# A two-layer decoder trunk on one core: an opening of small ordered transfers, first products in parts, six unread products, and weight casts kept in written order

## The chip, the core and the metric

The kernel runs on one core of a Trainium2 chip. Five engines work side by side, each on its own queue in the order in which its instructions stand: PE multiplies matrices, DVE and ACT work element by element, SP (and here at times ACT) issues transfers, POOL does almost nothing. An instruction waits at the head of its engine's queue until the semaphores that it needs are there, and all behind it wait too. The metric is the device time of one execution in microseconds (us).

## The reference, cut to what matters

256 tokens of width 2048 go through two layers, a pooling mixer and a latent attention, each followed by a gated embedding.

```python
h = x
for i in range(DEPTH):                       # DEPTH = 2
    xn = rms_norm(h, pre_norm[i])
    if i % 2 == 0:
        out = pool_mixer(xn, pool_w_in[j], pool_w_group[j], pool_scale[j], pool_w_out[j])
    else:
        out = mla_mixer(xn, cos, sin, mla_w_in[j], ...)
    h = h + rms_norm(out, post_norm[i])
    gate = jax.nn.sigmoid(rms_norm(h, ple_norm[i]) @ ple_w_gate[i])
    h = h + (p[i] @ ple_w_proj[i]) * gate
```

`pool_mixer` multiplies by `w_in` (2048 x 8192), averages over windows of 2, 4, 8 and 16 tokens, mixes in four groups, gates and multiplies by `w_out`. Everything is float32.

## The kernel before, in words

**Numbers in two parts.** To keep float32 accuracy on a faster multiplication, every operand is split: `hi` is the value rounded to fp32r, `lo` the rest. A product is `hi*x_hi + hi*x_lo` (one instruction of 512 columns, since x_hi and x_lo lie side by side) plus `lo*x_hi` (256 columns).

**Weights.** The 3248 weight tiles of 128 x 128 lie in memory in the order of their use, eight to a chunk, so 406 chunks, called c0 to c405 here. `Weights.load` (L188) brings a chunk into one of four `raw` buffers with one transfer (two for c0 and c1). `cut` rounds it on ACT into the upper half of one of eight `hl` buffers; `finish` subtracts on DVE for the lower half. When `take` reaches a new chunk, it emits further loads and casts; a cast is written up to six chunks ahead of use, and `W.rate` says how many are written at each new chunk. A load waits until the subtraction of four chunks earlier has freed its buffer.

**Order.** A list scheduler lays down the instructions of each engine. PE's products always keep their written order. ACT and DVE keep it only where `in_order(True)` is in force: in the opening and around the changes of stage. Elsewhere the scheduler may bring a cast forward, past evacuations that are written earlier.

**Opening.** The input x lies transposed in 16 tiles x0 to x15 of 128 x 256. The first stage takes 16 steps k, each with four output columns m: `split` makes x_k's hi (ACT) and lo (DVE) with the gain column from `vs`, and eight products follow. So one chunk serves two steps. The transfers of x0, `vs`, c0, x1, x2 and x3, c1 and so on are issued by SP, those of x8 to x15 by ACT between its other work.

**After it.** Columns m = 4, 5 and 6 of the same stage follow as whole rows of 32 products each (two chunks). Between them the sum of squares becomes `rstd` (two transposes on PE, copied by ACT). Until `rstd` is there, seven columns wait in the eight PSUM buffers. Then `pooled` (L381) takes each: an ACT copy, and on DVE an add, a product with rstd into `u`, the window sums `win`, an edge product, the mean `tmp`, and the split (ACT cast, DVE subtraction). The gate stage of each layer (at the end of `mixer_end`) has the same form: eight columns wait for its rstd, and each then takes an add, two products and an add on DVE and a sigmoid on ACT, in layer 0 also a split for the next layer.

**End.** The last column m = 15 of the last gate needs c404 and c405; `linear_short` takes three products of 256 columns for each of 16 tiles.

Of the kernel before, what the change touches and what calls it, by code (L numbers as in the profile page):

```python
# [9 lines left out]
F32 = mybir.dt.float32  # L10
F32R = mybir.dt.float32r
I32 = mybir.dt.int32
AF = mybir.ActivationFunctionType
ALU = mybir.AluOpType
AX = mybir.AxisListType

P = 128
D = 2048
T = 256
KD = D // P  # L20
# [16 lines left out]
CH = 8  # L37
SLOTS = 52
N_TILES = 3248
KO_POOL = 4  # L40
RUN = 16
KO_GATE = 5
N_FREE = 2
KO_LAT = 5
# [71 lines left out]


@with_exitstack
def tile_trunk(ctx: ExitStack, tc: tile.TileContext, ws, xp, pp, pos, vec, cst, outT):
    nc = tc.nc  # L120
    n_chunks = ws.shape[0]

# [1 line left out]
    wp = ctx.enter_context(tc.tile_pool(name="wp", bufs=1))  # L124
# [5 lines left out]
    def nm(s):  # L130
        uid[0] += 1
        return f"{s}_{uid[0]}"
# [13 lines left out]
            return emit  # L146

    pe, act, dve = InOrder(nc.tensor, True), InOrder(nc.scalar, False), InOrder(nc.vector, False)

    def in_order(on):  # L150
        act.on = dve.on = on

    def act_tile(dt=F32R):
        return ap.tile([P, 2 * T], dt, tag="act", name=nm("act"), bufs=SLOTS)
# [14 lines left out]
    def tmp_tile():  # L169
        return own_tile("tmp", 6)  # L170

    def ps_tile():
        return psp.tile([P, 2 * T], F32, tag="ps", name=nm("ps"))

    class Weights:
# [10 lines left out]
            self.rate = 2  # L186

        def load(self):  # L188
            c = self.loaded
            self.loaded += 1  # L190
            t = self.raw[c] = wp.tile([P, CH * P], F32, tag="raw", name=nm("raw"), bufs=4)
            for r in self.pieces(c):
                nc.sync.dma_start(t[:, r], ws[c][:, r])  # L193

        def cut(self):

            c = self.cut_to
            self.cut_to += 1
            hl = self.hl[c] = wp.tile([P, 2, CH * P], F32R, tag="hl", name=nm("hl"), bufs=8)
            for r in self.pieces(c):  # L200
                act.copy(hl[:, 0, r], self.raw[c][:, r])
            self.finish(c - 1)

        def finish(self, c):
            t = self.raw.pop(c, None)
            if t is not None:
                hl = self.hl[c]
                for r in self.pieces(c):
                    dve.tensor_tensor(hl[:, 1, r], t[:, r], hl[:, 0, r].bitcast(F32), ALU.subtract)

        def pieces(self, c):
            n = 2 if c < 2 else 1
            s = CH * P // n
            return [slice(i * s, (i + 1) * s) for i in range(n)]

# [6 lines left out]
        def take(self, *tiles):  # L222
            c, j = divmod(len(self.order), CH)
            n = len(tiles)
            assert j + n <= CH
            if j == 0:
                self.hl.pop(c - 1, None)
                while self.loaded < min(n_chunks, c + self.AHEAD_LOAD + 1):
                    self.load()
                while self.cut_to <= c:  # L230
                    self.cut()
                self.finish(c)
                self.run_ahead(self.rate)
            self.order += tiles
            r = slice(j * P, (j + n) * P)
            return self.hl[c][:, 0, r], self.hl[c][:, 1, r]

    W = Weights()

    vs = one.tile([P, NV], F32, name="vs")  # L240
    cs = one.tile([P, NK], F32, name="cs")
    ident = cs[:, K_ID : K_ID + P]
    ones = one.tile([P, P], F32, name="ones")
# [6 lines left out]
    def col(i):  # L250
        return vs[:, i : i + 1]

    def split(src, gain=None):
        t = act_tile()
        if gain is None:
            act.copy(t[:, :T], src)
            dve.tensor_tensor(t[:, T:], src, t[:, :T].bitcast(F32), ALU.subtract)
        else:
            act.activation(t[:, :T], src, AF.Copy, scale=gain)
            dve.scalar_tensor_tensor(  # L260
                t[:, T:], src, gain, t[:, :T].bitcast(F32), ALU.mult, ALU.subtract
            )
# [12 lines left out]
    def linear(xs, name, m, between=None):  # L275

        ps = ps_tile()
        n = len(xs)
        for a in range(0, n, RUN):
            burst(  # L280
                [(ps, xs[k], (name, k, m), k == 0, k == n - 1) for k in range(a, min(n, a + RUN))],
                between if a + RUN >= n else None,
            )
        return ps
# [16 lines left out]
    def outer_step(pss, x, name, k, n):  # L301
        burst([(ps, x, (name, k, m), k == 0, k == n - 1) for m, ps in enumerate(pss)])

    def whole(ps, out):
        t = tmp_tile()
        act.copy(t, ps[:, T:])
        dve.tensor_tensor(out, ps[:, :T], t, ALU.add)
        return out
# [46 lines left out]

    in_order(True)
    W.rate = 0
    early = one.tile([P, 1], F32, name="early")
    act.activation(early, mean_d, AF.Copy, scale=mean_r)
    x_t = []  # L360

    def load_x(queue, j):
        t = act_tile(F32)
        x_t.extend([t[:, :T], t[:, T:]])
        queue.dma_start(t, xp[:, 2 * j : 2 * j + 2, :])  # L365

    t = act_tile(F32)
    x_t += [t[:, :T], t[:, T:]]
    nc.sync.dma_start(t[:, :T], xp[:, 0, :])  # L369
    nc.sync.dma_start(vs, vec)  # L370
    W.load()
    nc.sync.dma_start(t[:, T:], xp[:, 1, :])  # L372
    for j in range(1, 4):
        load_x(nc.sync, j)
        W.load()

    u_buf = [one.tile([P, PAD + T], F32, name=f"u{i}") for i in range(2)]
    for t in u_buf:
# [30 lines left out]
        return s  # L409

    xs, pss = [], [ps_tile() for _ in range(KO_POOL)]
    for k in range(KD):
        xs.append(split(x_t[k], col(V_PRE[0] + k)))
        outer_step(pss, xs[k], "pool_in", k, KD)
        if len(x_t) < D // P:
            load_x(act, len(x_t) // 2)
        if k == KD // 2:
            nc.sync.dma_start(cs, cst)
        if k == 12:
            W.rate = 1  # L420
    acc = [own_tile("acc", 4) for _ in range(2)]
# [8 lines left out]
    for g in range(4):  # L430
# [18 lines left out]
        for i in range(8):  # L449
            ps = linear(pl, f"mix{g}", i)  # L450
            t = whole(ps, tmp_tile())
# [41 lines left out]
    def mixer_end(layer, src, h, pss):  # L493
# [43 lines left out]
        for i in range(KD + 2):  # L537
# [11 lines left out]
            if i >= 2:  # L549
                k = i - 2  # L550
                if k == 0:
                    pss = [ps_tile() for _ in range(KO_GATE)]
                dve.scalar_tensor_tensor(
# [50 lines left out]
    h, xs = mixer_end(0, gated, None, [])  # L604
# [12 lines left out]
    pss = [ps_tile() for _ in range(KO_LAT)]  # L617
# [37 lines left out]
    t = whole(linear(xs, "kpe", 0), tmp_tile())  # L655
# [131 lines left out]
    pss = None  # L787
# [9 lines left out]
    for i in range(H + 4):  # L797
# [5 lines left out]
        else:  # L803
            if i == H:
                pss = [ps_tile() for _ in range(KO_OUT)]
# [47 lines left out]
```

## Time and profile before

| what | us |
|---|---|
| median of 3 runs (1186.89 to 1188.99) | 1187.14 |
| the profiled execution's own time | 1186.3 |
| its span, first to last instruction | 1184.5 |
| PE busy | 1173.6 |
| PE's first product starts at | 5.86 |
| PE's last products end at | 1179.85 |

A row of a timeline gives the start, the time, the engine, the line, the operation, out<-in with the names of the program, the shapes, how many instructions are merged, and in brackets the idle time before it and what ended that. A row of a table of stretches gives from:to, the length, then busy us and (x) the instructions of PE, PEld, DVE, ACT and POOL, then the granted clock of PE (1.00 is the upper of its two levels), the DMA engines' busy share and GB/s. A row of the waits gives who waits, for whom, the total, how often, and the longest. Nearly all work stands at L142, the helper that records each operation, so rows are told apart by their tiles: `hl<-raw` is the work on weights, `act<-act,vs` a split with a gain, `ps` a PSUM buffer.

### The profile page before, as it was taken

Reading aid. Unit: us, or ns where it says so; the run is one execution under the profiler, and the core shown is the slowest. Engines: PE = TensorE matmul, PEld = TensorE weight load, DVE = VectorE, ACT = ScalarE, POOL = GpSimd, SP = SyncE. Lnnn points to the kernel's source line nnn. Section 1 sums busy time; section 2 is a strip of 40 time slices with the busy share of each in tenths; the row PEclk is TensorE's granted clock in tenths of the full one; section 3 lists DMA queues with packets and bytes.
Section 4 is the critical chain, followed back from the end, with each engine's and each line's share of the span. In section 5 each row is a group of like instructions: output and inputs, shape, how many; then the busy total and the mean of one; then the engine's idle time right before and its main releaser. Section 6 shows DMA issues by size and latency. Waiting matters only on the chain.

```text
span 1184.5 us, 18609 instructions
## 1 busy us (share of the span) xinstructions
PE 1173.6 (99%) x6928; PEld 1042.1 (88%) x6928; DVE 882.5 (75%) x1651; ACT 691.7 (58%) x1240; POOL 1.2 (0%) x10
## 2 busy tenths in 40 slices
PE   7999999999999999999999999999999999999998
PEld 6888888888888888888889889888888889889887
DVE  6888885788588866447446999678788897656995
ACT  7657454554554455445444776557787775655762
POOL 0000000000000000000000000000000000000000
PEclk9999999999999999999999999999999999999999
DMA  8766655655665665675662676655555443562681
GB/s 297 250 210 196 185 189 182 198 189 180 195 192 181 193 198 182 200 268 181 190 196 95 196 252 198 190 178 170 193 188 179 141 124 127 183 193 97 196 275 45
DMA packets 64363, 221.30 MB, mean 187 GB/s; under 512 B 7153, under 2 KB 9841, under 8 KB 64273
## 3 DMA queue, kind: packets, MB, share of 16 engines
q1 hardware_dynamic: 63648, 218.94, 58.4%
q8 instruction: 54, 0.88, 0.3%
q10 hardware_dynamic: 576, 1.05, 0.2%
q14 instruction: 37, 0.29, 0.1%
q0 software_dynamic: 48, 0.13, 0.0%
HBM read 217.99 MB, written 2.10 MB: 186 GB/s over the span
## 4 chain that ended last, share of the span: by engine, by line
PE 97%; DVE 1%; DMA 1%; ACT 0%; SPq 0%; issue 0%; ACTq 0%; DVEq 0%
PE ps L142 97%; DMA raw<-ws 1%; DVE act L142 1%; DVE hl L142 0%; ACT hl L142 0%; SPq L193 0%; SPq L365 0%; DVE tmp L142 0%; ACT tmp L142 0%; ACT act L142 0%; DVE mx L142 0%; SPq L372 0%; SPq L370 0%; SPq L369 0%; ACTq L142 0%
## 5 line engine op out<-in xcount | busy, mean ns | idle before, releaser
L142 PE MATMUL ps<-act,hl 128*128 128x256 f32 (+1 forms) x6512 | 1120.5, 334 | 6.0 <-ACT hl L142 5.9
L142 PEld LDWEIGHTS ps<-act,hl 128*128 128x128 f32 x6512 | 989.0, 190 | 131.7 <-ACT hl L142 6.2
L142 DVE TENSOR_TENSOR hl<-raw,hl 128x1024 fp32r<-128x1024 f32 (+1 forms) x408 | 493.6, 1217 | 223.8 <-ACT hl L142 222.2
L142 ACT CAST hl<-raw 128x1024 fp32r<-128x1024 f32 (+1 forms) x408 | 421.9, 1045 | 282.2 <-PE ps L142 252.7
L142 ACT COPY tmp<-ps 128x256 f32<-128x256 f32 x221 | 80.4, 368 | 61.6 <-PE ps L142 61.4
L142 DVE TENSOR_TENSOR tmp<-ps,tmp 128x256 f32<-128x256 f32 x155 | 64.7, 420 | 16.0 <-ACT tmp L142 15.4
L142 ACT ACTIVATE act<-act,vs 128x256 fp32r<-128x256 f32 (+1 forms) x102 | 50.8, 507 | 27.9 <-DVE act L142 23.3
L142 ACT CAST act<-tmp 128x256 fp32r<-128x256 f32 (+1 forms) x96 | 39.1, 407 | 25.0 <-DVE tmp L142 23.0
L142 DVE TENSOR_TENSOR acc<-acc,tmp 128x256 f32<-128x256 f32 x92 | 35.9, 421 | 14.1 <-ACT tmp L142 13.9
L142 ACT ACTIVATE tmp<-act 128x256 f32<-128x256 f32 x90 | 34.5, 414 | 14.1 <-DVE act L142 14.0
L142 ACT ACTIVATE act<-tmp 128x256 f32<-128x256 f32 x48 | 19.8, 416 | 36.7 <-DVE tmp L142 36.5
L142 DVE TENSOR_TENSOR act<-tmp,act 128x256 fp32r<-128x256 f32 (+1 forms) x96 | 40.2, 419 | 0.9
L142 DVE SCALAR_TENSOR_TENSOR act<-act,vs,act 128x256 fp32r<-128x256 f32 x72 | 33.8, 481 | 6.2 <-ACT act L142 6.2
L142 DVE TENSOR_TENSOR tmp<-tmp,rstd 128x256 f32<-128x256 f32 x74 | 30.9, 420 | 0.3
L142 PE MATMUL ps<-act,act 128*128 128x256 f32 (+1 forms) x224 | 30.6, 291 | 0.0
L142 DVE TENSOR_TENSOR act<-ps,tmp 128x256 f32<-128x256 f32 x66 | 27.3, 419 | 3.4 <-ACT tmp L142 3.1
L142 PEld LDWEIGHTS ps<-act,act 128*128 128x128 f32 x224 | 27.3, 190 | 0.3 <-DVE act L142 0.2
L142 DVE TENSOR_TENSOR act<-act,tmp 128x256 f32<-128x256 f32 (+1 forms) x65 | 26.7, 416 | 0.1
L142 PE MATMUL ps<-hl,act 128*128 128x512 f32 x96 | 22.5, 390 | 0.0
L142 DVE TENSOR_TENSOR win<-win 128x269 f32<-128x269 f32 (+2 forms) x48 | 20.9, 435 | 1.3
L142 PEld LDWEIGHTS ps<-hl,act 128*128 128x128 f32 x96 | 17.8, 188 | 3.5
L142 ACT COPY act<-ps 128x256 f32<-128x256 f32 (+2 forms) x52 | 17.9, 357 | 3.8 <-PE ps L142 3.5
(64 smaller groups left out, 300.3 us busy)
## 6 DMA issues: line engine op xcount, KB each, us to landing
raw<-ws SPq DMA_DIRECT2D x404, 512.0 KB, 4.0
act<-xp SPq DMA_DIRECT2D x11, 256.0 KB, 6.1
outT<-act SPq DMA_DIRECT2D x15, 128.0 KB, 1.7
raw<-ws SPq DMA_DIRECT2D x4, 256.0 KB, 4.2
act<-xp ACTq DMA_DIRECT2D x4, 256.0 KB, 7.2
act<-pp SPq DMA_DIRECT2D x2, 256.0 KB, 4.7
act<-xp SPq DMA_DIRECT2D x2, 128.0 KB, 3.3
cs<-cst SPq DMA_DIRECT2D x1, 206.0 KB, 7.6
```

Source lines behind the costliest of these rows:

```text
L142: i = getattr(self.engine, op)(*a, **k)
```

## The change

The casts and subtractions of weights go through two recorders of their own (`w_act`, `w_dve`) that are always in written order. SP's opening transfers are in written order too. x0 and all gains come in one array `first`, issued by ACT: first x0 with its gain column, then all columns into `vs`. All of x now goes by SP, between the chunks. c0 comes in four pieces, c1 to c5 in two each, and c0 to c5 land in twelve tiles of the pool of activations, so that the four `raw` buffers start with c6. For c0 and c1 the casts and subtractions are written where their products need them, c0's first two casts on DVE. Step 0 is written in parts: hi with x_hi, hi with x_lo, then lo. Ahead of it six products of a tile of ones go to a PSUM buffer that is not read.

```diff
+N_BORROW = 6
+N_HALVED = 2
+N_WARM = 6
...
+    sp = InOrder(nc.sync, True)
+    w_act, w_dve = InOrder(nc.scalar, True), InOrder(nc.vector, True)
...
         def load(self):
             c = self.loaded
             self.loaded += 1
-            t = self.raw[c] = wp.tile([P, CH * P], F32, tag="raw", name=nm("raw"), bufs=4)
-            for r in self.pieces(c):
-                nc.sync.dma_start(t[:, r], ws[c][:, r])
+            if c < N_BORROW:
+                slots = [act_tile(F32) for _ in range(2)]
+                parts = [slots[r.start // (4 * P)][:, r.start % (4 * P) :][:, : r.stop - r.start] for r in self.pieces(c)]
+            else:
+                t = wp.tile([P, CH * P], F32, tag="raw", name=nm("raw"), bufs=4)
+                parts = [t[:, r] for r in self.pieces(c)]
+            self.raw[c] = parts
+            for r, t in zip(self.pieces(c), parts):
+                sp.dma_start(t, ws[c][:, r])
...
-            for r in self.pieces(c):
-                act.copy(hl[:, 0, r], self.raw[c][:, r])
+            if c < N_HALVED:
+                return
+            for r, t in zip(self.pieces(c), self.raw[c]):
+                w_act.copy(hl[:, 0, r], t)
             self.finish(c - 1)
 
         def finish(self, c):
...
+            for r, t in zip(self.pieces(c), self.raw.pop(c, ())):
+                w_dve.tensor_tensor(self.hl[c][:, 1, r], t, self.hl[c][:, 0, r].bitcast(F32), ALU.subtract)
...
         def pieces(self, c):
-            n = 2 if c < 2 else 1
+            n = 4 if c == 0 else 2 if c < N_BORROW else 1
...
+    act.dma_start(x0[:, : T + 1], first[:, : T + 1])
+    act.dma_start(vs, first[:, T:])
...
+    for j in range(1, KD // 2):
+        load_x(j)
         W.load()
+    sp.dma_start(cs, cst)
+    sp.on = False
+    warm = ps_tile()
+    for _ in range(N_WARM):
+        pe.matmul(warm[:, :P], ones, ones, start=True, stop=True)
...
+        for i in range(2):
+            W.first_part(0, i, dve.tensor_copy)
+        gain = x0[:, T : T + 1]
+        act.activation(x[:, :T], x_t[0], AF.Copy, scale=gain)
+        dve.scalar_tensor_tensor(x[:, T:], x_t[0], gain, x[:, :T].bitcast(F32), ALU.mult, ALU.subtract)
+        for i in range(2):
+            W.second_part(0, i)
+        for h in range(2):
+            for ps, (hi, _) in zip(pss, steps):
+                pe.matmul(ps[:, h * T : h * T + T], hi, x[:, h * T : h * T + T], start=h == 0, stop=False)
+        for ps, (_, lo) in zip(pss, steps):
+            pe.matmul(ps[:, :T], lo, x[:, :T], start=False, stop=False)
```

PE's order is the same from step 1 to the end. ACT's and DVE's is not, in the whole program. Three places follow.

The first is ACT behind the first `rstd`, before the change. `CAST hl` rows are chunks: hl_522 is c18, hl_656 is c19, hl_659 c20; `COPY tmp` and `CAST act` belong to `pooled`.

```order
L142 CAST hl_522<-raw_447 128x1024
L142 CAST hl_656<-raw_452 128x1024
L142 COPY rstd_544<-ps_541 128x256
L142 CAST hl_659<-raw_515 128x1024
L142 CAST hl_664<-raw_520 128x1024
L142 COPY tmp_576<-ps_102 128x256
L142 CAST act_572<-tmp_570 128x256
L142 CAST hl_715<-raw_654 128x1024
```

The same place after the change, where hl_558 is c18 and hl_692 is c19; the four pairs of `COPY tmp` and `CAST act` that are left out are of the columns between.

```order
L145 CAST hl_558<-raw_483 128x1024
L145 COPY rstd_580<-ps_577 128x256
L145 COPY tmp_612<-ps_139 128x256
L145 CAST act_608<-tmp_606 128x256
...
L145 COPY tmp_677<-ps_550 128x256
L145 CAST act_673<-tmp_671 128x256
L145 COPY tmp_736<-ps_689 128x256
L145 CAST act_686<-tmp_684 128x256
L145 CAST hl_692<-raw_488 128x1024
L145 CAST hl_695<-raw_551 128x1024
```

The cast of c19 stood ahead of rstd's copy; now it stands behind the split of all seven columns that waited for rstd. DVE there goes from one column to the next without a subtraction of weights in between: its last `TENSOR_TENSOR hl` before the seven is c17's.

The second is ACT in layer 0's gate, behind the copy of its second rstd: before the change, where hl_7048 is c249.

```order
L142 CAST hl_6922<-raw_6847 128x1024
L142 COPY rstd_6944<-ps_6941 128x256
L142 CAST hl_7048<-raw_6852 128x1024
L142 COPY tmp_6979<-ps_6404 128x256
L142 COPY tmp_6990<-ps_6405 128x256
L142 CAST hl_7051<-raw_6915 128x1024
L142 ACT_TABLE_LOAD
```

And after it, where hl_7084 is c249; the 24 rows left out are copies, sigmoids, splits and squares of eight columns.

```order
L145 CAST hl_6958<-raw_6883 128x1024
L145 COPY rstd_6980<-ps_6977 128x256
L145 COPY tmp_7015<-ps_6440 128x256
L145 COPY tmp_7026<-ps_6441 128x256
L145 ACT_TABLE_LOAD
...
L145 ACTIVATE act_7077<-act_5304,vs 128x256
L145 CAST hl_7084<-raw_6888 128x1024
```

c249's cast went from the place right behind rstd to the place behind the split of the eighth column. On DVE 39 instructions of these columns (33 of them TENSOR_TENSOR, 6 SCALAR_TENSOR_TENSOR) stand from rstd to the sum that this split reads.

The third is DVE at the end. Before the change the subtraction of the last chunk c405 (hl_12313) stands among the work of columns 9 to 12.

```order
L142 TENSOR_TENSOR tmp_12097<-act_11438,tmp_12097 128x256
L142 TENSOR_TENSOR tmp_12204<-tmp_12204,rstd_12013 128x256
L142 TENSOR_TENSOR hl_12313<-raw_12263,hl_12313 128x1024
L142 TENSOR_TENSOR tmp_12256<-ps_12257,tmp_12300 128x256
L142 TENSOR_TENSOR tmp_12152<-act_11438,tmp_12152 128x256
```

After the change c405 is hl_12349.

```order
L145 TENSOR_TENSOR tmp_12434<-ps_12435,tmp_12468 128x256
L145 TENSOR_TENSOR tmp_12434<-tmp_12434,rstd_12049 128x256
L145 TENSOR_TENSOR tmp_12434<-act_11878,tmp_12434 128x256
L145 TENSOR_TENSOR act_5312<-act_5312,tmp_12434 128x256
L145 TENSOR_TENSOR hl_12349<-raw_12299,hl_12349 128x1024
L145 TENSOR_TENSOR tmp_12476<-ps_12477,rstd_12049 128x128 x2
```

It moved behind the four instructions of column 14, the last but one, which wait for that column's products.

## Rows read from the trace of the kernel before

**Rows 1.** The page, busy time of each engine, share of the span, instructions.

```profile
PE 1173.6 (99%) x6928; PEld 1042.1 (88%) x6928; DVE 882.5 (75%) x1651; ACT 691.7 (58%) x1240; POOL 1.2 (0%) x10
```

**Rows 2.** Waits of PE's weight loads: who, for whom, total, times, longest.

```profile
PEld ps L142 <- ACT hl L142: 6.2, 2, 5.9
PEld ps L142 <- DVE act L142: 1.0, 4, 0.3
```

**Rows 3.** Timeline of the opening, all engines.

```profile
3.23 0.51 ACT L142 ACTIVATE act<-act,vs 128x256 fp32r<-128x256 f32 x1 [0.90 <-DMA vs<-vec]
...
5.19 1.32 ACT L142 CAST hl<-raw 128x512 fp32r<-128x512 f32 x2 [1.46 <-DMA raw<-ws]
...
5.86 34.16 PE L142 MATMUL ps<-act,hl 128*128 128x512 f32 x176 [5.86 <-ACT hl L142]
...
6.94 0.51 ACT L142 ACTIVATE act<-act,vs 128x256 fp32r<-128x256 f32 x1 [0.43 <-DMA act<-xp]
```

**Rows 4.** Two stretches of 3.4 us: busy time and instructions of each engine, clock, DMA.

```profile
5.86:9.26 3.40, 3.40 (x10) 2.92 (x11) 2.58 (x5) 2.43 (x5) 0.00 (x0) 1.00 0.86 270
9.26:12.66 3.40, 3.40 (x20) 2.92 (x20) 1.70 (x4) 1.47 (x4) 0.00 (x0) 1.00 1.03 402
```

**Rows 5.** ACT's timeline at the first rstd.

```profile
45.78 1.05 ACT L142 CAST hl<-raw 128x1024 fp32r<-128x1024 f32 x1 [0.24 <-DMA raw<-ws]
47.05 1.05 ACT L142 CAST hl<-raw 128x1024 fp32r<-128x1024 f32 x1 [0.21 <-DMA raw<-ws]
48.00 0.36 ACT L142 COPY rstd<-ps 128x256 f32<-128x256 f32 x1
```

**Rows 6.** PE's timeline: the transposes of the first rstd.

```profile
45.88 0.38 PE L142 MATMUL ps<-cs,small 128*128 128x128 f32 x2
```

**Rows 7.** Two stretches from a rstd on, columns as in rows 4.

```profile
46.00:60.98 14.98, 14.98 (x91) 13.35 (x90) 13.56 (x24) 9.03 (x14) 0.00 (x0) 1.00 0.77 258
688.92:703.89 14.97, 14.97 (x91) 13.35 (x90) 14.42 (x26) 13.26 (x24) 0.00 (x0) 1.00 0.78 265
```

**Rows 8.** Timeline of pooled columns, ACT and DVE.

```profile
54.02 0.42 DVE L142 TENSOR_TENSOR tmp<-ps,tmp 128x256 f32<-128x256 f32 x1
54.14 0.41 ACT L142 CAST act<-tmp 128x256 fp32r<-128x256 f32 x1 [1.36 <-DVE tmp L142]
54.45 1.04 ACT L142 CAST hl<-raw 128x1024 fp32r<-128x1024 f32 x1
...
55.81 0.43 DVE L142 SCALAR_TENSOR_TENSOR tmp<-win,u 128x256 f32<-128x256 f32 x1
56.16 1.22 DVE L142 TENSOR_TENSOR hl<-raw,hl 128x1024 fp32r<-128x1024 f32 x1
...
59.09 0.42 DVE L142 TENSOR_TENSOR u<-tmp,rstd 128x256 f32<-128x256 f32 x1
...
60.56 1.22 DVE L142 TENSOR_TENSOR hl<-raw,hl 128x1024 fp32r<-128x1024 f32 x1
```

**Rows 9.** ACT's timeline behind layer 0's second rstd.

```profile
689.20 0.37 ACT L142 COPY rstd<-ps 128x256 f32<-128x256 f32 x1 [0.42 <-PE ps L142]
...
692.55 1.28 ACT L142 ACT_TABLE_LOAD   x1
693.85 0.73 ACT L142 ACTIVATE tmp<-tmp 128x256 f32<-128x256 f32 x2
```

**Rows 10.** DVE's timeline a few us later.

```profile
701.06 0.42 DVE L142 TENSOR_TENSOR tmp<-ps,tmp 128x256 f32<-128x256 f32 x1
701.39 0.88 DVE L142 SCALAR_TENSOR_TENSOR act<-act,vs,act 128x256 fp32r<-128x256 f32 x2
```

**Rows 11.** Timeline of the end, ACT and DVE.

```profile
1174.17 0.37 ACT L142 COPY tmp<-ps 128x256 f32<-128x256 f32 x1 [3.88 <-PE ps L142]
...
1176.41 0.43 DVE L142 TENSOR_TENSOR act<-act,tmp 128x256 f32<-128x256 f32 x1
1179.88 0.49 DVE L142 TENSOR_TENSOR tmp<-ps,rstd 128x128 f32<-128x128 f32 x2 [3.04 <-PE ps L142]
```

More of the change, by code (lines that the diff above doesn't have):

```diff
@@ L118, in tile_trunk @@
 @with_exitstack
-def tile_trunk(ctx: ExitStack, tc: tile.TileContext, ws, xp, pp, pos, vec, cst, outT):
+def tile_trunk(ctx: ExitStack, tc: tile.TileContext, ws, xp, first, pp, pos, cst, outT):
     nc = tc.nc
@@ L199, in cut, with first_part, second_part @@
             hl = self.hl[c] = wp.tile([P, 2, CH * P], F32R, tag="hl", name=nm("hl"), bufs=8)
-            for r in self.pieces(c):
-                act.copy(hl[:, 0, r], self.raw[c][:, r])
+            if c < N_HALVED:
+                return
+            for r, t in zip(self.pieces(c), self.raw[c]):
+                w_act.copy(hl[:, 0, r], t)
             self.finish(c - 1)
         def finish(self, c):
[L205 to L209, printed above, removed]
+            if c < N_HALVED:
+                return
+            for r, t in zip(self.pieces(c), self.raw.pop(c, ())):
+                w_dve.tensor_tensor(self.hl[c][:, 1, r], t, self.hl[c][:, 0, r].bitcast(F32), ALU.subtract)
+        def first_part(self, c, i, copy):
+            copy(self.hl[c][:, 0, self.pieces(c)[i]], self.raw[c][i])
+        def second_part(self, c, i):
+            r = self.pieces(c)[i]
+            dve.tensor_tensor(self.hl[c][:, 1, r], self.raw[c][i], self.hl[c][:, 0, r].bitcast(F32), ALU.subtract)
         def pieces(self, c):
-            n = 2 if c < 2 else 1
+            n = 4 if c == 0 else 2 if c < N_BORROW else 1
             s = CH * P // n
@@ L233, in take @@
                 self.run_ahead(self.rate)
+            if 0 < c < N_HALVED and j % (CH // 2) == 0:
+                self.first_part(c, j // (CH // 2), act.copy)
+                self.second_part(c, j // (CH // 2))
             self.order += tiles
@@ L357, in tile_trunk, with load_x @@
     W.rate = 0
+    x0, t = act_tile(F32), act_tile(F32)
+    act.dma_start(x0[:, : T + 1], first[:, : T + 1])
+    act.dma_start(vs, first[:, T:])
     early = one.tile([P, 1], F32, name="early")
     act.activation(early, mean_d, AF.Copy, scale=mean_r)
-    x_t = []
-    def load_x(queue, j):
+    x_t = [x0[:, :T], t[:, T:]]
+    def load_x(j):
         t = act_tile(F32)
         x_t.extend([t[:, :T], t[:, T:]])
[L365 to L370, printed above, removed]
+        sp.dma_start(t, xp[:, 2 * j : 2 * j + 2, :])
     W.load()
-    nc.sync.dma_start(t[:, T:], xp[:, 1, :])
-    for j in range(1, 4):
-        load_x(nc.sync, j)
+    sp.dma_start(t[:, T:], xp[:, 1, :])
+    for j in range(1, KD // 2):
+        load_x(j)
         W.load()
+    sp.dma_start(cs, cst)
[3 more added lines that the diff above has]
+        pe.matmul(warm[:, :P], ones, ones, start=True, stop=True)
     u_buf = [one.tile([P, PAD + T], F32, name=f"u{i}") for i in range(2)]
@@ L411, in tile_trunk, with first_step @@
     xs, pss = [], [ps_tile() for _ in range(KO_POOL)]
+    def first_step():
+        x = act_tile()
+        steps = [W.take(("pool_in", 0, m)) for m in range(KO_POOL)]
+        for i in range(2):
[10 more added lines that the diff above has]
+            pe.matmul(ps[:, :T], lo, x[:, :T], start=False, stop=False)
+        return x
     for k in range(KD):
+        if k == 0:
+            xs.append(first_step())
+            continue
         xs.append(split(x_t[k], col(V_PRE[0] + k)))
+        if k == 1:
+            for i in range(2, 4):
+                W.first_part(0, i, act.copy)
+                W.second_part(0, i)
         outer_step(pss, xs[k], "pool_in", k, KD)
[L415 to L418, printed above, removed]
         if k == 12:
@@ L834 @@
         "xp": np.ascontiguousarray(a["x"][0].T.reshape(KD, P, T).transpose(1, 0, 2)),
+        "first": np.ascontiguousarray(np.concatenate([a["x"][0].T[:P]] + [vec(x) for x in vecs], 1)),
         "pp": np.ascontiguousarray(a["p"][:, 0].transpose(0, 2, 1).reshape(2, 2, P, T).transpose(0, 2, 1, 3)),
         "pos": np.ascontiguousarray(a["positions"].reshape(T)),
-        "vec": np.ascontiguousarray(np.concatenate([vec(x) for x in vecs], 1)),
         "cst": _consts(),
```

## The prediction

> **What bounds the kernel now.** I read the page first: PE is busy 1173.6 of a span of 1184.5 us [rows 1]. The reader should see that all other time is to be found in about 11 us, so I looked for each idle stretch of PE. The table of waits shows two of its weight loads waiting for a cast of weights, together 6.2, the longest 5.9; that is the start of the program, with 0.3 a little later. Four waits for DVE's `act`, 1.0 in all, stand in the attention [rows 2]. The timeline of the opening shows why PE starts at 5.86: x0's split could go only at 3.23, behind `vs`, and c0's first cast at 5.19, behind its transfer [rows 3]. The stretches behind it show a second loss: PE is busy throughout both, yet does 10 products in the first 3.40 us and 20 in the next. [...] Last comes the tail: PE's last products end just before 1179.88, and DVE and ACT finish up to 1184.5 [rows 1, 11]. So there is little to win, and anything that makes PE wait for ACT or DVE costs its full length.
>
> **The opening.** New are a transfer of x0 with its gain column, a first quarter of c0, and hi/lo products apart. Today data that were issued first were there by 3.23 [rows 3]; a split takes 0.51 [rows 3], so PE's first product can stand at about 3.7, against 5.86: 2.2 earlier. With the wait of 0.3 behind it [rows 2], which the quarters should end, G = 2.4. The lower end is 1.0: the first stretch moved only 270 GB/s against 402 in the next [rows 4], and the bytes ahead of x1, whose split ran at 6.94 on arrival [rows 3], are as many as before, so a start at 3.7 may buy waits at steps 1 and 2. [...]
>
> **Place 1, the cast of c19.** The rows of the order show it moved behind the splits of all seven columns that waited for rstd. PE's order is unchanged, and c19's first product stood at 60.98: 91 products lie from 46.00 to it, the first three of them already begun [rows 7]. When can it stand now? I count from DVE's first `u` behind rstd. The rest of the first column takes 60.56 - 59.09 = 1.47, a whole column 56.16 - 54.02 = 2.14, and six follow. The last column's split needs its STT, which starts 0.35 before the column's end and takes 0.43; ACT's split passes to the next cast after 0.31, and a cast takes 1.05 [rows 5, 8]. A hand-over between engines I estimate at 0.04, twice. 1.47 + 12.84 - 0.35 + 0.43 + 0.31 + 1.05 + 0.08 = 15.8.
>
> The clock of that sum starts at rstd's copy, which has to wait for two things. One is the transposes: 45.88 + 0.38 = 46.26 today [rows 6], minus G after the change. With 0.04 + 0.36 + 0.04, u stands at 46.70 - G and the product at 62.5 - G: a loss of 1.5 - G against 60.98. The other is c18's cast, which stands ahead of the copy on ACT. Today it began at 45.78 after waiting for its transfer, and its successors follow 0.95 later (47.05 to 48.00) [rows 5]. If it begins D earlier, the copy starts at 46.73 - D, u at 47.13 - D and the product at 62.95 - D: a loss of 2.0 - D. The larger of the two holds. So the opening's gain is kept only if c18's transfer moves with it. That transfer waits for a buffer that c14's subtraction frees, and so back by fours to c6, which starts free now. Each link still has a transfer, a cast and a subtraction that the change does not shorten. D lies between -0.7 (c14's cast now queues behind a copy of 0.36 and a split of 0.31 [rows 5, 8]) and 2.4 (it moves with PE). I choose 0.7, nearer to the end at which the transfer sets the pace, since that is what the row of 45.78 names. Net: 2.0 - 0.7 = **+1.3**, from -0.9 (1.5 - 2.4) to +2.7. It is the position of PE after both opening and wait; the wait itself would be G + 1.3 = 3.7 long.
>
> **Place 2, the cast of c249.** The copy of rstd ran at 689.20 for 0.37, so DVE begins at 689.61 [rows 9]. The 39 instructions ahead of the split: 33 at 0.33 (701.06 to 701.39), and 6 at 0.40 (two in 0.88, less 0.09 of overlap) [rows 10], 10.9 + 2.4 = 13.3. After four of them, at 690.9, DVE needs the first sigmoid: on ACT two copies (0.3 each, between a copy's 0.37 and a split's 0.31), the table load of 1.28 and a sigmoid of 0.42 (0.73 for two [rows 9]) follow the rstd copy, to 691.9. That is 1.0 of waiting. 689.61 + 13.3 + 1.0 = 703.9; then the split 0.51 [rows 3], the cast 1.05 [rows 5] and hand-overs 0.08, 705.5. Needed is 703.89 [rows 7]. PE waits **1.6**, counted from the same rstd, so that nothing earlier or later in the program changes it. Bounds: 0.6 if the sigmoid is not waited for, 2.2 if DVE waits half a table load, 0.6, once more among ACT's other 24 instructions.
>
> **Attention.** Some weight subtractions now stand behind the scalings of the softmax, so `act` for PE may come earlier or weights later. What waits there today is 1.0 [rows 2]. I take 0, bounds -1.0 and +1.0 (the same wait, changed to weights).
>
> **Place 3, the end.** The subtraction of c405 stands behind column 14's last add, 1176.41, which passes on after 0.33 [rows 10, 11]; with 1.22 of its own [rows 8] it ends at 1177.97 and PE can go on at 1178.0. The 48 products of column 15 took from the copy of column 14 (1174.17) to DVE's first read (1179.88), 0.119 each [rows 11]. The first product began about 0.2 before that copy; 24 for c404 and two of hi later c405's lower half is needed at 1173.97 + 26 x 0.119 = 1177.1. PE waits **0.9** (0.7 to 1.0), with nothing behind it to hide that.
>
> Everywhere else the casts are written up to six chunks ahead of PE, so that a few places' shift on ACT (58% busy) or DVE (75%) [rows 1] lies behind PE's products: 0.
>
> **Sum.** 1.3 + 1.6 + 0 + 0.9 = +3.8. The profiled execution took 1186.3, so 1190.1; the median, 1187.14, lies 0.84 above that execution, and I keep that: **1190.9**. A measurement of this kernel can tell about 0.2%, 2.4 us, from no change.
>
> **The rivals.**
>
> *The early start survives place 1* (not slower). If the borrowed tiles let c6 to c18 come as much earlier as PE does, D is over 2.05, rstd's copy goes with the transposes, and place 1 gives 1.5 - 2.4 = -0.9. Then -0.9 + 1.6 + 0.9 = +1.6: 1188.7, within 0.2%. For it: the cast of c18 waited only for a transfer [rows 5], and the DMA engines were 0.77 busy there [rows 7]. Against it: three buffers' rounds lie between.
>
> *The columns are quicker than rows 8 say* (faster). Then neither place 1 nor 2 waits and G stays: -2.4 - 1.0 (attention) + 0.9 = -2.5, 1184.6. It needs 3.7 us less in seven columns, 0.5 of 2.14 each; the six DVE instructions of a column fill 2.0 at 0.33 each [rows 10], which speaks strongly against.
>
> *The clock falls back.* The first products ran at half pace after PE had idled for 5.86 [rows 3, 4]. Were a wait of 3.7 at place 1 enough for that, 1.7 comes on top: 1192.6. The waits of up to 0.3 that the trace has elsewhere [rows 2] don't decide it. [...]
>
> *The opening doesn't deliver.* If waits at steps 1 and 2 eat the start, G is about 0 and the transposes would give place 1 +1.5, but D is then near 0, so place 1 gives 2.0 and the sum is 2.0 + 1.6 + 0.9 = +4.5: 1191.6. For it: the low DMA rate of the first stretch [rows 4]. Against it: x1's transfer has no more bytes ahead than today.
>
> **How the numbers follow.** Forecast 0.50 (its own range 1189.3 to 1192.5, of it 0.05 within 0.2%); early start survives 0.24; clock falls back 0.10; opening doesn't deliver 0.09; quicker columns 0.07. Faster: 0.07. Within 0.2%: 0.24 + 0.05 = 0.29. Slower: 0.45 + 0.10 + 0.09 = 0.64. For the range, the bounds that can come together: low, the early start with 1.6 less for the attention and place 2 together, 1187.1; high, the clock case with 1.2 more at the places, 1193.8. I write 1187.0 to 1193.8; the quick columns and the tails left out hold under 2 in 10.
>
> **What would show it.** Right: a first product at about 3.7; one wait of PE for a cast near 58 to 62 of some 3.7 us, whose chunk's cast on ACT stands right behind a split; one near 705 of 1.6; one for DVE's `hl` of 0.9 just before the last products. If the copy of rstd runs well before 46, the early start survives. Ten instead of twenty products in the 3.4 us behind the wait show the clock. The forecast is wrong if ACT's casts there wait for nothing, if the wait at place 1 is missing, or if the opening starts later than 4.6.

## The result and the profile after

The changed kernel took 1194.46 us (median, 1193.44 to 1197.6) against 1187.09 of the kernel before: ratio 1.0066, 95% interval 1.0055 to 1.0078, so 7.4 us slower. The prediction was 1190.9 in a range of 1187.0 to 1193.8: the right direction, half of the size, and outside the range. Its first profiled execution took 1197.6, the longest of the four; a second profiled execution of the same code, told among the experiments, took 1193.6. I read both, since they differ in what matters.

The waits of PE's weight loads in the changed kernel, to be set against [rows 2]:

```profile
PEld ps L145 <- ACT hl L145: 10.0, 4, 4.9
PEld ps L145 <- DVE act L145: 1.3, 5, 0.6
PEld ps L145 <- DVE hl L145: 1.0, 1, 1.0
```

The 5.9 of the start is gone, yet casts cost more than before: two long waits in the middle of the program. The wait for a lower half (`DVE hl`) is the one at the end. The kernel before had one such wait too, in a row that [rows 2] leave out; it lay in the opening, at 14.62:

```profile
PEld ps L142 <- DVE hl L142: 0.5, 1, 0.5
```

The opening in the timeline, against [rows 3]:

```profile
3.56 0.51 ACT L145 ACTIVATE act<-act 128x256 fp32r<-128x256 f32 x1 [0.31 <-DMA act<-first]
...
4.12 2.64 PE L145 MATMUL ps<-act,hl 128*128 128x256 f32 x12 [0.20 <-ACT act L145]
...
5.91 0.51 ACT L145 ACTIVATE act<-act,vs 128x256 fp32r<-128x256 f32 x1 [1.84 <-DMA act<-xp]
...
7.08 3.22 PE L145 MATMUL ps<-act,hl 128*128 128x512 f32 x16 [0.31 <-ACT hl L145]
...
10.45 0.62 ACT L145 CAST hl<-act 128x512 fp32r<-128x512 f32 x1 [1.46 <-DMA act<-ws]
...
11.12 2.14 PE L145 MATMUL ps<-act,hl 128*128 128x512 f32 x10 [0.82 <-ACT hl L145]
```

PE starts at 4.12 instead of 5.86, but then waits for casts ahead of 7.08 and 11.12; the cast at 10.45 had itself waited for the second half of c1, where the kernel before had cast all of c1 by 9.52:

```profile
8.38 1.14 ACT L142 CAST hl<-raw 128x512 fp32r<-128x512 f32 x2
```

The transposes of the first rstd tell what is left. They stood at 45.88 [rows 6] and now start at 45.39, so 0.5 us of the gain remains:

```profile
45.39 0.40 PE L145 MATMUL ps<-cs,small 128*128 128x128 f32 x2 [0.22 <-issue]
```

ACT around the first rstd, against [rows 5] (the left-out rows are the columns' copies and splits):

```profile
45.50 1.05 ACT L145 CAST hl<-raw 128x1024 fp32r<-128x1024 f32 x1 [3.50 <-DMA raw<-ws]
46.73 1.05 ACT L145 CAST hl<-raw 128x1024 fp32r<-128x1024 f32 x1 [0.19 <-DMA raw<-ws]
47.94 1.06 ACT L145 CAST hl<-raw 128x1024 fp32r<-128x1024 f32 x1 [0.15 <-DMA raw<-ws]
48.90 0.36 ACT L145 COPY rstd<-ps 128x256 f32<-128x256 f32 x1
...
63.76 0.41 ACT L145 CAST act<-tmp 128x256 fp32r<-128x256 f32 x1 [1.46 <-DVE tmp L145]
64.07 2.94 ACT L145 CAST hl<-raw 128x1024 fp32r<-128x1024 f32 x3
```

The three casts at the top are c16, c17 and c18, each on the arrival of its transfer. c18 began at 47.94, 2.16 later than before the change; rstd's copy stands right behind it, and c19's cast (64.07) behind the seventh split.

Two more rows tell where a part of this delay comes from: the cast of c8, and the issue of c18's load by SP. First the changed kernel, then the kernel before, where c8 is the second of the two casts and starts at 23.77.

```profile
25.53 1.05 ACT L145 CAST hl<-raw 128x1024 fp32r<-128x1024 f32 x1 [1.97 <-DMA raw<-ws]
...
41.18 0.33 SPq L145 DMA_DIRECT2D raw<-ws  x1
```

```profile
22.84 1.99 ACT L142 CAST hl<-raw 128x1024 fp32r<-128x1024 f32 x2
...
40.54 0.33 SPq L193 DMA_DIRECT2D raw<-ws  x1
```

c18's load went out 0.64 later than before, and 6.76 passed from its issue to the cast instead of 5.24.

PE behind c19's cast, and stretches of 3.4 us behind it, against [rows 7]:

```profile
65.17 1.22 PE L145 MATMUL ps<-act,hl 128*128 128x512 f32 x2 [4.48 <-ACT hl L145]
```

```profile
65.17:68.57 3.40, 3.40 (x8) 2.72 (x9) 3.40 (x5) 2.11 (x3) 0.00 (x0) 0.50 0.40 93
68.57:71.97 3.40, 3.40 (x19) 3.26 (x19) 3.33 (x8) 1.45 (x2) 0.00 (x0) 0.62 0.90 322
```

c19's first product stood at 60.98 and now stands at 65.17: +4.19. Behind the wait of 4.48 the granted clock is 0.50, the lower of the two values that it takes in this trace: it reads 1.00 from 60 to 64.0, 0.50 from 64.5 to 70.67, and 1.00 again from 71.17. In the first 3.4 us PE is busy all the time and does 8 products.

ACT at layer 0's gate, against [rows 9]:

```profile
696.92 1.05 ACT L145 CAST hl<-raw 128x1024 fp32r<-128x1024 f32 x1 [0.66 <-DMA raw<-ws]
697.87 0.36 ACT L145 COPY rstd<-ps 128x256 f32<-128x256 f32 x1
...
712.75 0.51 ACT L145 ACTIVATE act<-act,vs 128x256 fp32r<-128x256 f32 x1 [0.56 <-DVE act L145]
713.17 2.93 ACT L145 CAST hl<-raw 128x1024 fp32r<-128x1024 f32 x3
```

PE's row there:

```profile
714.25 0.96 PE L145 MATMUL ps<-act,hl 128*128 128x512 f32 x3 [3.18 <-ACT hl L145]
```

Before the change this copy waited for PE ([rows 9], "0.42 <-PE ps"). Now it comes directly behind a cast (c248) that waited for its transfer.

The end, against [rows 11], DVE and then PE:

```profile
1186.55 0.42 DVE L145 TENSOR_TENSOR act<-act,tmp 128x256 f32<-128x256 f32 x1
1186.90 1.22 DVE L145 TENSOR_TENSOR hl<-raw,hl 128x1024 fp32r<-128x1024 f32 x1
1191.10 0.49 DVE L145 TENSOR_TENSOR tmp<-ps,rstd 128x128 f32<-128x128 f32 x2 [2.98 <-PE ps L145]
```

```profile
1188.17 2.89 PE L145 MATMUL ps<-act,hl 128*128 128x256 f32 x22 [0.82 <-DVE hl L145]
```

The subtraction of c405 follows column 14's add after 0.35, and PE waits 0.82 for it.

### The profile page after: what moved, and what is told of

Its sections match the earlier page's. It is cut to its first block, busy times and chain, and to the rows that moved or that the text cites. A ratio compares the mean times of both kernels' runs of the same rounds, so it can differ in the third digit from the quotient of the medians.

```text
span 1195.7 us, 18457 instructions
## 1 busy us (share of the span) xinstructions
PE 1179.6 (99%) x6944; PEld 1046.9 (88%) x6944; DVE 887.9 (74%) x1659; ACT 693.1 (58%) x1244; POOL 1.2 (0%) x10
## 4 chain that ended last, share of the span: by engine, by line
PE 88%; DVE 5%; DMA 3%; ACT 2%; issue 1%; SPq 0%; DVEq 0%; ACTq 0%
PE ps L145 88%; DMA raw<-ws 2%; DVE act L145 2%; DVE tmp L145 2%; DVE hl L145 1%; ACT hl L145 1%; ACT tmp L145 1%; DMA act<-ws 1%; DMA act<-xp 0%; DVE win L145 0%; ACT act L145 0%; DVE acc L145 0%; DVE u L145 0%; DMA act<-first 0%; ACT L145 0%
## 5 line engine op out<-in xcount | busy, mean ns | idle before, releaser
L145 DVE TENSOR_TENSOR hl<-raw,hl 128x1024 fp32r<-128x1024 f32 x400 | 479.9, 1220 | 47.7 <-ACT hl L145 46.9
L145 ACT CAST hl<-raw 128x1024 fp32r<-128x1024 f32 x400 | 408.8, 1046 | 103.9 <-DMA raw<-ws 82.0
L145 ACT ACTIVATE tmp<-act 128x256 f32<-128x256 f32 x90 | 34.3, 413 | 16.3 <-DVE act L145 15.2
L145 ACT ACTIVATE tmp<-tmp 128x256 f32<-128x256 f32 (+1 forms) x33 | 13.2, 407 | 13.8 <-DVE tmp L145 13.8
```

The costliest lines, as they stand in the source:

```text
L145: i = getattr(self.engine, op)(*a, **k)
```

## The experiments

Medians are of 4 to 12 executions; the kernel before, measured beside each, stood at 1187.0.

### The changed kernel once more

The same code, for a second profile.

> The changed kernel once more, unaltered, for a second profile. Theory (c19's product stands 17.2 behind the start of c18's cast and c249's 16.3 behind the copy of its rstd; what differs from run to run is when c18 and c248 land): both distances hold within 0.2 us although the landings differ by 1 us or more from the first profile; 1193 to 1195. Rival (the first profile's late landing at 47.9 is the program's own): c18 is cast at 47.9 again, within 0.3.

1193.60 us, ratio 1.0059 (1.0046 to 1.0072). ACT at the first rstd, then PE at the three places:

```profile
46.37 1.05 ACT L145 CAST hl<-raw 128x1024 fp32r<-128x1024 f32 x1 [0.69 <-DMA raw<-ws]
47.32 0.37 ACT L145 COPY rstd<-ps 128x256 f32<-128x256 f32 x1
```

```profile
63.58 2.81 PE L145 MATMUL ps<-act,hl 128*128 128x512 f32 x9 [3.40 <-ACT hl L145]
...
710.26 2.11 PE L145 MATMUL ps<-act,hl 128*128 128x512 f32 x8 [1.97 <-ACT hl L145]
...
1184.30 2.89 PE L145 MATMUL ps<-act,hl 128*128 128x256 f32 x22 [0.82 <-DVE hl L145]
```

```profile
63.70:67.10 3.40, 3.40 (x14) 2.90 (x15) 3.40 (x5) 1.99 (x3) 0.00 (x0) 0.69 0.43 120
```

c18's cast began 1.57 earlier than in the first profile, and c19's product came 17.21 behind it (17.23 in the first). At the gate the copy of rstd ran at 693.90 and c249's product 16.36 behind it (16.38 in the first). Three more executions with the written order, told below, have 17.22 and 17.23 at the first place, and all three 16.38 at the gate. So both distances are the program's, and the time of the cast ahead of them is what differs between executions. The rival is out. In this profile c18's load was issued at 40.99, and 5.38 passed to its cast.

### The opening without the written order

```diff
-    w_act, w_dve = InOrder(nc.scalar, True), InOrder(nc.vector, True)
+    w_act, w_dve = act, dve
```

> The changed kernel, but casts and subtractions of weights may again be brought forward by the scheduler as before the change; the new opening stays. Theory (the written order costs the time, in three places, and the clock after the first): none of the three waits is there, and what is left is the 0.5 us by which PE was ahead at 59 us in the changed kernel, so 1186 to 1187, ratio 0.999 to 1.000. Rival (the opening itself delays the transfers of c6 to c18, and PE pays for that in any order): PE waits for a cast before 65 us, 1188.5 or more.

1191.35 us, ratio 1.0039 (1.0026 to 1.0052): the time lies where the rival had it, but the reason is another. None of the three waits is there, and no transfer came late: c18's cast starts at 44.63, 1.15 earlier than in the kernel before. PE waits elsewhere. DVE, then PE and the stretch behind its wait:

```profile
45.70 1.23 DVE L145 TENSOR_TENSOR hl<-raw,hl 128x1024 fp32r<-128x1024 f32 x1 [3.17 <-ACT hl L145]
46.84 0.15 DVE L145 SCALAR_TENSOR_TENSOR small<-small,small 128x2 f32<-128x2 f32 x1
46.94 1.23 DVE L145 TENSOR_TENSOR hl<-raw,hl 128x1024 fp32r<-128x1024 f32 x1
48.08 0.15 DVE L145 SCALAR_TENSOR_TENSOR small<-small,small 128x2 f32<-128x2 f32 x1
```

```profile
48.34 0.66 PE L145 MATMUL ps<-cs,small 128*128 128x128 f32 x2 [3.35 <-issue]
```

```profile
48.30:51.70 3.40, 3.36 (x18) 3.39 (x19) 2.98 (x4) 1.29 (x2) 0.00 (x0) 0.58 0.90 294
```

The scheduler put the subtractions of c18 and c19 between the last steps of rstd's Newton iteration (`small`). The first of them stands at the head of DVE's queue and waits 3.17 for c18's cast, which had to wait for its transfer; PE's transposes wait for the iteration, and the clock falls behind that wait (0.58). "issue" as their releaser is misleading: the row of DVE that ends at 48.23 shows who was late.

### The written order without the opening

In the kernel before, the cast in `cut` and the subtraction in `finish` go through `w_act` and `w_dve`, as in the change.

```diff
+    w_act, w_dve = InOrder(nc.scalar, True), InOrder(nc.vector, True)
-                act.copy(hl[:, 0, r], self.raw[c][:, r])
+                w_act.copy(hl[:, 0, r], self.raw[c][:, r])
-                    dve.tensor_tensor(hl[:, 1, r], t[:, r], hl[:, 0, r].bitcast(F32), ALU.subtract)
+                    w_dve.tensor_tensor(hl[:, 1, r], t[:, r], hl[:, 0, r].bitcast(F32), ALU.subtract)
```

> The kernel before, with only the casts and subtractions of weights kept in written order; the old opening. Theory (order): waits of PE at the same three places; c18 is cast near 45.8, so place 1 costs 2.0, place 2 1.6 to 3.4, the end 0.9 to 1.1; 1191.5 to 1193.5, and the clock does not fall at place 1 since the wait is 2 and not 4.5. Rival (the late c18 came from the order, not from the opening): place 1 costs 4 and the clock falls there too, 1195 to 1198.

1193.17 us, ratio 1.0050 (1.0038 to 1.0062): the theory's size. So the written order alone costs 6.2 us without the new opening. PE's row at place 1 and the stretch behind it:

```profile
64.02 1.20 PE L142 MATMUL ps<-act,hl 128*128 128x512 f32 x4 [2.37 <-ACT hl L142]
```

```profile
64.02:67.42 3.40, 3.40 (x21) 3.06 (x22) 3.40 (x5) 2.12 (x3) 0.00 (x0) 1.00 0.39 105
```

c19's product is 3.04 late, half-way between theory (2.0) and rival (4), since c18 was cast at 46.78 here and not near 45.8, with 17.23 between them. The clock stayed at 1.00, as the theory had it, and 21 products went in 3.4 us, where the changed kernel did 8 and 14. Place 2 cost a wait of 2.40 and the end one of 0.82.

### The casts of c19 and c20 written earlier

`one_ahead` writes one more cast ahead of the first rstd's copy:

```diff
             def bcast():
                 nonlocal rs
+                W.run_ahead(1)
                 [rs] = next(st)
```

> The changed kernel with one cast more written ahead of the first rstd's copy, so c19 stands before the seven columns and c20 is the first behind them. Theory: rstd's copy comes about 1.2 later (c19 lands at 49.1), c20 is cast at some 66.3 and its products are due 3.7 after those of c19, 64.2: a wait of about 2.1 instead of 4.5, and the clock stays: 3 to 5 us faster than the changed kernel's profiled 1197.6, 1191 to 1193. Rival (any chunk behind the seven columns waits the same, and the clock falls by any such wait): within 1 us of the changed kernel.

1193.15 us, ratio 1.0048 (1.0036 to 1.0060): not decided by its time, since the changed kernel's own second run took 1193.60. In its profile PE waits for neither cast, only 0.33 for c19's lower half; the expected 2.1 was too much, as c19 was cast at 46.66 and not after 49.1, and so the columns behind it began earlier. But place 2 cost 2.22 of waiting, and the clock fell there (0.60 in the next 3.4 us).

`pin_mend` keeps the written order and writes two more casts behind the copy of rstd, at the first rstd and at the gates (`rs2`):

```diff
                 [rs] = next(st)
+                W.run_ahead(2)
                 W.rate = 2
...
             [rs2] = next(st)
+            W.run_ahead(2)
             W.rate = 2
```

> The changed kernel, all in written order, but at the first rstd and at the gates two more casts (c19 and c20; c249 and c250) are written right behind the copy of rstd, ahead of the columns. Theory (it is the place of these two casts that costs): the waits at places 1 and 2 shrink to 0 to 1.5 each, the clock stays, the end keeps its 0.9; 1188 to 1190.5. Rival (whatever is written behind the columns waits as long): 1193 or more.

1189.51 us, ratio 1.0023 (1.0015 to 1.0031), as expected, though two of the twelve executions took 1191.91 and 1193.62. In its profile the wait at place 1 is gone; at the gate a wait of 0.58 for a lower half is left, and the 0.82 at the end is there. It is 4.1 us below the second run of the changed kernel, with nothing else altered, so most of the loss hangs on the place of these casts.

### PE kept busy through place 1

Sixteen unread products of the tile of ones stand between c18's and c19's upper products.

```diff
-        for ps, x, (hi, _), first, _ in steps:
+        for i, (ps, x, (hi, _), first, _) in enumerate(steps):
+            if len(W.order) == 20 * CH and i == CH:
+                idle = ps_tile()
+                for _ in range(N_FILL):
+                    pe.matmul(idle[:, :P], ones, ones, start=True, stop=True)
             pe.matmul(ps, hi, x, start=first, stop=False)
```

> The changed kernel with 16 unread products of the tile of ones on PE between the upper products of c18 and those of c19, where it waits at place 1; at full pace they take 3.4 us, which is within the wait. Theory (the clock falls in that wait and costs up to 2.8 us): the granted clock stays at 1.00 after place 1, PE does about 20 products in the 3.4 us behind it, and the time is 1191.5 to 1192.5, 2 to 3 under the changed kernel. Rival (the half pace has no part in the typical run): 1194 to 1195.

1192.39 us, ratio 1.0059 (1.0045 to 1.0072). PE's row and the stretch that starts just before c19's first product at 63.67:

```profile
59.99 3.74 PE L146 MATMUL ps<-ones 128*128 128x128 f32 x32
63.67 6.52 PE L146 MATMUL ps<-act,hl 128*128 128x512 f32 x35
```

```profile
62.90:66.30 3.40, 3.40 (x22) 2.95 (x21) 3.40 (x6) 2.89 (x4) 0.00 (x0) 1.00 0.16 41
```

In the trace the theory holds: c19's product still stands 17.22 behind c18's cast (46.45); c19's cast ends at 63.63, so it sets that start and not the unread products, which take 3.74 instead of the expected 3.4 and end at about the same time. But the clock stays at 1.00. The time is 1.2 us below that of the changed kernel's second run, and the intervals overlap, so the runs alone would not show it.

### One engine's weight work in written order

ACT alone, and then DVE alone:

```diff
-    w_act, w_dve = InOrder(nc.scalar, True), InOrder(nc.vector, True)
+    w_act, w_dve = InOrder(nc.scalar, True), dve
```

> The changed kernel with only the casts (ACT) in written order; subtractions (DVE) go where the scheduler puts them. Theory (rstd's copy stands behind c18's cast, c19's cast behind seven splits, whatever DVE does): place 1 has c19's product 17.2 us behind the start of c18's cast, place 2 a wait of 1.5 to 3.5, the end none: 1191 to 1194. Rival (the subtractions held back on DVE are the cause): no wait over 1 us at the two places, 1188 or less.

1200.89 us, ratio 1.0116 (1.0102 to 1.0130), more than both theories. It has the fault of the opening alone (3.7 at the transposes) and, at the gate, that of the written casts. Behind both waits the clock falls (0.50 and 0.52 in the 3.4 us behind them; the mean over this profile's 1199.7 us is 0.994):

```profile
PE ps L145 <- ACT hl L145: 4.4, 3, 3.5
PE ps L145 <- issue: 3.7, 1, 3.7
PE ps L145 <- DVE act L145: 3.0, 5, 1.2
```

```diff
-    w_act, w_dve = InOrder(nc.scalar, True), InOrder(nc.vector, True)
+    w_act, w_dve = act, InOrder(nc.vector, True)
```

> The changed kernel with only the subtractions (DVE) in written order; c19's cast stands ahead of rstd's copy again. Theory: at the two places PE has its upper halves and waits for a lower half (DVE hl) by about 1 at most each, and 0.9 at the end: 1188 to 1190. Rival (subtractions cost as much as casts): waits of 2 or more at the two places, 1192 or more.

1245.60 us, ratio 1.0492 (1.0478 to 1.0507). Both expectations are far off:

```profile
PE ps L145 <- DVE hl L145: 41.8, 22, 4.9
```

```profile
ACT hl L145 <- DMA raw<-ws: 357.3, 246, 7.6
```

PE waits 22 times for a lower half, all through the program, and ACT's casts wait 246 times for a transfer (22 times, 19.6 in all, in the kernel before); a buffer for one comes free only by a subtraction. That evacuations brought forward on ACT then stand behind casts that wait is my reading; I did not test it.

### Without the six unread products

`N_WARM = 0` in the changed kernel.

> The changed kernel without the six unread products. Theory: the half pace then lasts up to about 7.5 us instead of 6.2, but PE waits at 6.8 and 10.3 for data anyway and place 1 is set by c18's transfer: same as the changed kernel within 1 us. Rival (the half pace is paid in full): 1 to 1.7 us slower than the changed kernel.

1193.23 us, ratio 1.0052 (1.0040 to 1.0065): 0.4 below the changed kernel's second run and 1.2 below its first, so nothing measurable is lost without the six products, as the theory had it. c18 was cast at 45.55 in its profile, c19's product came 17.23 later, PE waited 2.57 and the clock stayed (1.00 in the 3.4 us behind it). The theory's 7.5 us is an estimate: PE's first product at 4.1, and the 3.40 us of [rows 4].

### The opening with rstd's chain mended

The scheduler is free again, and the casts of c19 and c20 are written behind the copy of the first rstd, so that the subtractions of c18 and c19 are written there too and no longer get into the Newton iteration.

```diff
-    w_act, w_dve = InOrder(nc.scalar, True), InOrder(nc.vector, True)
+    w_act, w_dve = act, dve
...
                 [rs] = next(st)
+                W.run_ahead(2)
                 W.rate = 2
```

> The new opening, the scheduler free to bring casts and subtractions forward as before the change, and the casts of c19 and c20 written right behind the copy of the first rstd, which leaves DVE's chain for rstd unbroken. Theory (the 3.4 us of the run with the opening alone came from a subtraction put into that chain, which waited for a late cast): that wait is gone, no other place waits over 0.5, and 1185.5 to 1187 comes out, equal to or up to 1.5 below the kernel before. Rival (the opening makes c16 to c18 late for any order): a wait of 1.5 or more stays near 46 to 62, 1188.5 or more.

1185.31 us, ratio 0.9986 (0.9977 to 0.9995): below both kernels, and the lowest with the run that follows; it lies 0.2 under the expected range. The wait at the transposes is gone. All waits that PE has left are in the opening, one of them (0.8) above the 0.5 of the theory:

```profile
PE ps L145 <- POOL mean_r L271: 1.0, 1, 1.0
PE ps L145 <- ACT hl L145: 0.8, 1, 0.8
PE ps L145 <- ACT act L145: 0.2, 1, 0.2
```

The same with `N_WARM = 0`:

> The mended kernel without the six unread products. [...] Rival (they are worth the whole half pace): 1186.5 to 1187.

1185.11 us, ratio 0.9983 (0.9975 to 0.9992). The six products are worth nothing that can be measured, and the rival's 1186.5 to 1187 is not reached. PE starts at 4.09 in this profile and never waits again. In its second 3.4 us it is busy throughout and does 17 products, where the mended kernel with the six did 19 (7.50 to 10.90) and [rows 4] have 20. The granted clock reads 1.00 there, as it does in both stretches of [rows 4], so there is only the count to go by, and it does not show how long the slow start lasts.

```profile
7.49:10.89 3.40, 3.40 (x17) 2.87 (x17) 2.26 (x5) 1.91 (x5) 0.00 (x0) 1.00 1.02 337
```

## Why the prediction was half of the loss

A wait in PE's row is counted from the end of a product; products overlap by 0.16 (in the kernel before one of the 6512 with weights lasts 334 ns in the mean, and together they fill 1120.5 us, 172 ns each), so the delay is that much more. The delay of one and the same product against the kernel before, at the places of the prediction:

| | predicted | first profile | second profile |
|---|---|---|---|
| c19's first product (60.98 before) | +1.3 | +4.19 | +2.60 |
| half pace behind it | 0 | +2.83 | +1.64 |
| wait at place 2 | +1.6 | +3.34 | +2.13 |
| attention and the rest | 0 | -0.12 | -0.01 |
| wait at the end | +0.9 | +0.98 | +0.98 |
| sum, at DVE's first read of the last column | +3.8 | +11.22 | +7.34 |

Half pace is what is left at c249's product: 714.25 - 703.89 = 10.36, less 4.19 and 3.34; and 710.26 - 703.89 = 6.37, less 2.60 and 2.13. The sum is 1191.10 and 1187.22 (the same read in the second profile) less 1179.88. The second profile, 1193.6, is near the median and the one to judge by.

**Place 1: the mechanism and the distance were right, D had the wrong sign.** The prediction put c19's product 17.17 behind c18's cast (45.78 to 62.95). Measured: 17.21 to 17.23 in five executions of kernels with the written order. The 0.04 estimated for a hand-over is near the 0.03 that the trace of before has between x0's split on ACT, which ends at 3.74, and DVE's part of it at 3.77. The step that failed is "I choose 0.7" for D. c18's cast came not earlier but later: by 2.16 in the first profile, 0.59 in the second, and from 45.55 to 47.94 over those five.

Two parts add up to that. One is when c18's load goes out. The prediction followed its buffer "back by fours to c6, which starts free now", but c6's load went out at 14.36, against 14.59 before, so the borrowed tiles gave next to nothing there; and c8's cast, waiting for its transfer, came at 25.53 and 25.34 instead of 23.77. From there to the issue of c18's load ACT and DVE work in written order in every kernel here: 15.65 passed in both profiles and 15.65 to 16.00 in the nine other executions with this opening, with the scheduler free behind it or not. So that distance comes with the opening and not with the pinned casts. c8's own cast lies between 23.58 and 25.53 in these eleven; why its transfer lands so differently stays open. This part makes 0.64 of the 2.16 and 0.45 of the 0.59. The other part is the way from issue to cast: 6.76 and 5.38, against 5.24 before and 5.68 to 5.94 in the three other executions. Why that differs so much stays open: c16, c17 and c18 were issued 1.1 us after one another in all of them, as in the kernel before.

**The opening was over-estimated, and it did not matter, as forecast.** G was put at 2.4. Read at the transposes it was 0.49 in the first profile, 0.96 in the second and 1.33 in the mended kernel, whose median lies 1.7 us below the kernel before; the lower bound was 1.0. The step at fault is that bound, on steps 1 and 2: x1 is split at 5.91 instead of 6.94, but the second half of c1 is cast only at 10.45, where the kernel before had cast all of c1 by 9.52, and PE waits for it.

**The clock: a rival at 0.10 that came true.** The 3.4 us behind place 1 run at a granted 0.50 and 0.69 in the two profiles, with 8 and 14 products, where 21 are done at 1.00 behind the waits of 2.37 and 2.57 and 22 at 1.00 where PE was kept busy. The rival's 1.7 is an estimate, half of the 3.40 us of the first stretch of [rows 4], and no run shows a loss of just that; the runs showed 1.64 in the second profile and 2.83 in the first. Behind the shorter waits at place 1 in the profiles without unread products (2.57) and without the opening (2.37) the clock stayed at 1.00, so the price is not paid at every wait. I gave it 0.10 because no row of before showed a fall behind a wait. The wait of 3.7 that the forecast itself contained was a reason to give it more.

**Place 2: the distance was right, the start wrong.** 16.3 from rstd's copy was forecast, 16.36 to 16.38 measured in the same five executions. The step that failed is "counted from the same rstd, so that nothing earlier or later in the program changes it". In the row of before the copy waited for PE; I took that for granted and did not ask, as at place 1, which cast stands ahead of it on ACT. Moved by the delay that PE had by then, 2.60 + 1.64, the copy would have come at 693.4 in the second profile; it came at 693.9, behind c248's cast. In the first profile it was 1.65 late (697.87 against 689.20 + 7.02). That the start moves with earlier delays is no fault of the sum; that it moves further than they do is.

**The end and the attention: right.** 0.98 against 0.9, and nothing against nothing.

The rival on the other side, the early start that survives place 1, was mis-stated: by the prediction's own rule that the larger loss holds, -0.9 needs D above 2.9 and not 2.05, and D was bounded at 2.4, where place 1 gives -0.4. So its 1188.7 should have been 1189.2 at best. No execution came near: the largest D among the five was 0.23.

## What to carry to other kernels

- Where a cast moves behind a chain of evacuations, its time is the start of that chain plus a fixed length, which rows of before gave to a tenth of a us here (17.17 against 17.21 to 17.23, 16.3 against 16.36 to 16.38). The start depends on what stands ahead of the chain on the same engine; if that is work that waits for a transfer, count with the spread of the landings, and do so at each place of the same shape.
- A forecast wait of several us on PE should carry a price for a slow clock behind it: here 1.64 and 2.83 came on top of waits of 3.40 and 4.48, and nothing of the kind behind 2.37 and 2.57.
- Freedom of the scheduler costs too: a subtraction that waited 3.17 for a cast, and so for a transfer, got into a chain of small steps for which PE then waited 3.35. Writing two casts earlier there gave what pinning everything did not (1185.31 against 1193.60).

## What the runs showed of the hardware that was not expected

- The length of a wait alone does not say here whether the clock falls: it fell behind waits of 4.48 (changed kernel, place 1), 3.73 and 3.52 (the casts alone in written order), 3.40 (second profile, place 1), 3.35 (the opening alone) and 2.22 (c19 earlier, place 2) and stayed at 1.00 behind 3.18 (changed kernel, place 2), 2.57 (no unread products) and 2.37 (the written order alone). In the run with the casts alone in written order it also fell behind two waits of 1.19 and 0.72 close together (0.53).
- When it fell, the granted clock column showed it (0.50, 0.50, 0.52, 0.69, 0.58 and 0.60 in the 3.4 us behind these six, in this order); in the kernel before the column read 1.00 through 3.4 us in which PE did 10 products instead of 20 [rows 4].
- The same code cast the same chunk on arrival 1.6 us apart in two executions (c18 at 47.94 and 46.37). The issue of its load (41.18 and 40.99) makes 0.2 of that, and the way from issue to cast the rest.
- The changed kernel's times spread over 4 us in each of its two series (1193.44 to 1197.6 and 1192.23 to 1196.58), those of the mended kernel, whose PE does not wait for such a landing, over 1.5 (1184.85 to 1186.30). That the landings make the difference is likely, but not shown by itself.
